# Second products of the attention scores, and the delta rule's exponent rows, over 128 partitions padded with zeros

## The chip, the cores and the metric

The kernel runs on one core of a Trainium2 chip. The metric is the device time of one execution in microseconds (us). TensorE (PE in the profile) multiplies out of SBUF into PSUM. VectorE (DVE), ScalarE (ACT) and GpSimd (POOL) do the rest, and SyncE (SP) issues most of the transfers.

## The reference, cut to what matters

The program is two blocks of a network on 512 tokens of 1024 features: recurrence with forgetting attention, dilated and sliding attention, two cross attentions, MLPs, a gated delta rule, native sparse attention and two layers of experts, all in float32. The change touches two kinds of product in it.

```python
# forgetting, dilated, sliding and sparse attention: heads of 64 features, blocks of 128 queries
sc = jnp.einsum("bqhd,bkhd->bhqk", q[:, q0:q1], k[:, :q1]) * scale
...
p = jax.nn.softmax(jnp.where(mask, sc + bias, -jnp.inf), axis=-1)
outs.append(jnp.einsum("bhqk,bkhd->bqhd", p, v[:, :q1]))
...
# gated delta rule: the factors of a chunk's scores
decay = jnp.exp(jnp.where(causal, gc[..., :, None] - gc[..., None, :], -jnp.inf))
a_strict = einsum('bhncd,bhnsd->bhncs', k_beta, k) * decay
qk = einsum('bhncd,bhnsd->bhncs', q, k) * decay
```

## The kernel before, in words

A float32 value that goes through TensorE is kept as two parts, the rounded value and the rest. Linear layers (`lin_f`, `lin_1`, lines L151 to L153) contract 128 features at a time with three products of parts.

Attention works on one head and 128 queries at a time (j = 0 to 7: four blocks of queries in descending order, two heads). `q_parts` lays a head's rounded queries on one half of the 128 partitions of a tile Q and their rest on the other half. `k_parts` writes the rounded keys to both halves of K, so that one product over 128 partitions gives (rounded query + rest) times rounded key. The rounded query times the key's rest is a second product. Before the change the rests of two heads lie in one tile KL, each on its own 64 partitions, and this product contracts 64 partitions only:

```python
a = slice(e * 64, e * 64 + 64)
return [(Q[e][:, qs], K[e][:, ks]), (Q[e][a, qs], L[a, ks])]
```

`probs` (L294) issues these products into a PSUM bank of tag s (three banks), with a third product over 128 partitions (`crx` with `at`) in forgetting attention. VectorE then takes the minimum (L299, L300) and ScalarE the exponential with its sum (L302, out P). `pv` transposes P on TensorE (L310, into a bank o), copies it (L789 on VectorE or L787 on ScalarE, out PT), and multiplies it with the values (L314, into a bank pt).

The stages with this attention are `ab` (forgetting, 4 pairs of heads), `cd` (dilated and sliding, 8) and `nsa` (8 chunks in two branches, the selected blocks and the window): 32, 64 and 128 second products. The keys seen are 512, 384, 256 or 128 columns. Cross attention (`xa`) has heads of 256 features and contracts 128 partitions in every product.

In `gdn_group` (four groups) each of 4 chunks and 2 heads adds exponent rows to the mask in PSUM by a product that contracts 40 partitions, `gsel` with `rows` (L986, both named g_r in the trace): 32 products in all. Eight partitions from 0 and eight from 32 carry data and the rest are zeros.

The order on each engine comes from a list scheduler at build time, which runs the projections of the next pair of heads between the steps of the present one. Tiles are in rings by tag: x has 16 tiles of 1024 columns, t six of 512, h four. An engine keeps its order, so an instruction that waits holds all behind it.

Of the kernel before, what the change touches and what calls it, by code (L numbers as in the profile page):

```python
# [15 lines left out]
# tiles of the activations by tag: bytes of a row / 2048, and how many; each tag is a queue of its own  # L16
BUFS = {"t": 6, "x": 16, "h": 4, "y": 10, "P": 3, "PT": 3, "bc": 2, "ws": 4, "wh": 3, "wl": 3}
BANKS = {"lin": 2, "pt": 1, "s": 3, "o": 2}
S = 512
# [4 lines left out]
# the experts in the order they are computed in: three of each group of four, then the last of each  # L24
# [9 lines left out]
class Kern:  # L34
# [57 lines left out]
    def tconst(self, name, tag="y"):  # L92
        """A constant of [128, n] that lives in the tiles of the activations, until its last use."""
        src = self.A[name]
        n = src.shape[1]
        x = (self.t(name) if tag == "t" else self.T(name))[:src.shape[0], :n]
        self.nc.sync.dma_start(x, src)
        return x
# [17 lines left out]
    def raw(self, src):  # L116
        """A weight as it is, in the tiles of the weights."""
        self.uid += 1
        x = self.wp.tile([128, 1024], F32, tag="ws", name=f"raw_{self.uid}", bufs=BUFS["ws"])[:src.shape[0], :src.shape[1]]
        self.nc.sync.dma_start(x, src)  # L120
        return x
# [13 lines left out]
    def wap(self, name, kt, cols, off=0):  # L135
        """Pieces (tiles of rows, parts) of a weight that is laid out as [chunk][128][kt * cols]."""
# [11 lines left out]
    def mm3(self, out, a, b, start, stop):  # L148
        """out += a^T b from parts (h, l) of both."""
        mm = self.nc.tensor.matmul  # L150
        mm(out, a[0], b[0], start=start, stop=False)  # L151
        mm(out, a[0], b[1], start=False, stop=False)  # L152
        mm(out, a[1], b[0], start=False, stop=stop)  # L153

    def lin_f(self, w, chunks, xs, evac, N=S, cols=128):
        """Feature-major: evac(c, psum [cols, N]) for each chunk of columns."""
# [6 lines left out]
    def lin_t(self, w, chunks, xs, evac, cols=256, N=S):  # L163
        """Token-major: evac(c, t, psum [128, cols]) for each chunk and tile of tokens."""
# [11 lines left out]
    def lin_s(self, name, cols, xs, evac, put):  # L176
        """A few columns, by token: evac(dst [cols, S], psum), then put(t, psum [128, cols])."""
# [9 lines left out]
    def rms_prep(self, hT, gcol, N=S, scaled=True):  # L187
        """Split parts of h * g by tile, and a function that returns the root mean square's inverse by token and as
        a row on every partition, worked out at its first call."""
# [37 lines left out]
    def rsqrt(self, x, n):  # L227
        """1 / sqrt(x) of a small tile, x > 0: a guess from its bits and three steps of Newton's method."""
# [15 lines left out]
    def bcast(self, r, nt):  # L244
        """[128 tokens, nt] -> [128, nt * 128]: each token's value on every partition."""
# [11 lines left out]
    def q_parts(self, y, name="Q", scale=1.0):  # L257
        """Of each head a tile: its queries times scale, the rounded part where the head lies in y, the rest on the
        other 64 partitions."""
# [9 lines left out]

    def k_parts(self, y, L, name="K", tag="x"):  # L270
        """Of each head a tile with its rounded keys twice; the rest, as it lies in y, to L."""
        K = self.pair(name, tag, F32R)
        for e in range(2):
            a = slice(e * 64, e * 64 + 64)
            for b in range(2):
                self.nc.scalar.activation(K[e][b * 64:b * 64 + 64], y[a], AF.Copy)
            self.nc.vector.tensor_tensor(L[a], y[a], rd(K[e][a]), op=OP.subtract)
        return K

    def qk(self, Q, K, L, e, qs, ks):  # L280
        """The products of head e's queries and keys: of both parts with the rounded keys, and of the rounded
        queries with the keys' rest."""
        a = slice(e * 64, e * 64 + 64)
        return [(Q[e][:, qs], K[e][:, ks]), (Q[e][a, qs], L[a, ks])]

# [1 line left out]
    def probs(self, qk, nk, strip, mn, den, extra=None, floor=None):  # L287
        """exp(logits - max) of 128 queries, [128, nk], with the sums in den."""
# [35 lines left out]
    def pair_out(self, ob, ys):  # L324
        """The transpose of two heads' features of all the tokens, split, into ys; the tiles of tokens in descending
        order."""
# [6 lines left out]
    def out_f(self, name, off, ys, halves=(0, 1), chunks=range(8)):  # L333
        """The residual plus ys^T W, in two halves of ys: the first of them need not wait for the second."""
# [27 lines left out]
    def ab(self):  # L362
# [18 lines left out]
        # log of the forget gate, cumulated  # L381
# [16 lines left out]
        # the cumulated logs of 8 heads as seen from each tile of queries, 32 partitions each: the rounded parts and  # L398
        # after them the rest
        cr, (crh, crl) = self.t("cr"), self.rpair("crx")  # L400
# [13 lines left out]
        def proj(i):  # L414
            if i % 2 == 0:
                self.KL = self.rpair("KL")
            L = self.KL[i % 2]

            def ev(n, p):
                y = self.t("qk")  # L420
                if n < 8:
                    nc.vector.scalar_tensor_tensor(y, p, -0.125, rms()[1], op0=OP.mult, op1=OP.mult)
                    parts[i] = [self.q_parts(y), None, L]
                else:
                    nc.vector.tensor_tensor(y, p, rms()[1], op=OP.mult)
                    parts[i][1] = self.k_parts(y, L)
# [33 lines left out]
    def conv4(self, u, wc, bc):  # L460
        """Causal depthwise convolution of width 4."""
# [9 lines left out]
    def lru(self, uc):  # L471
        nc, vec, V = self.nc, self.vec, VCOL
        # 2 softplus(-lam) = -2 log sigmoid(lam), with a guard for very negative lam
# [12 lines left out]
        for j in range(4):  # L486
# [8 lines left out]
            # i * u, and b = (1 + a) s = 1 - a, with a = (1 - s) / (1 + s)  # L495
# [11 lines left out]
    def gelu(self, g):  # L507
        """2 gelu, tanh form."""
# [10 lines left out]
    def lru_out(self, hs, g, ys):  # L519
        """The scan's result times the gate."""  # L520
# [4 lines left out]
    def cd(self):  # L525
# [34 lines left out]
        def proj_k(i, n):  # L560
            if i % 2 == 0:
                self.KL = self.rpair("KL")
            L = self.KL[i % 2]

            def ev(n, p):
                kp[i] = self.k_parts(rotated(p, 1.0), L), L
# [13 lines left out]
        def sliding(i):  # L580
            """Heads i and i + 4, with sinks."""
# [48 lines left out]
    def mem_prep(self):  # L630
        """The memory, and a function that works out its root mean square's inverse."""
# [37 lines left out]
    def xa(self, l):  # L669
# [19 lines left out]
        for hp in range(2):  # L689
            # the transposed weights of two heads, in parts: [128 keys, block of keys, token]  # L690
# [81 lines left out]
    def row_const(self, name, n):  # L772
        """A row of a kernel input on every partition."""
# [9 lines left out]
    def copy(self, out, in_):  # L783
        """A copy out of PSUM by the scalar and the vector engine in turn."""
# [6 lines left out]
    def gdn(self):  # L791
# [4 lines left out]
        # a and b of each token and head  # L796
# [15 lines left out]
        # softplus(a) = max(a, 0) + log(1 + exp(-|a|)), the rounding of 1 + exp taken back  # L812
# [18 lines left out]
        # per token and head: beta / 2, -beta exp(gc), exp(gc), exp(gl - gc), gc; per head exp(gl);  # L831
        # rho: the exponents of a row of the scores, gc + log beta and gc
# [13 lines left out]
        # keys and queries are kept as 2 silu(), their norms go into the exponents and the factors  # L846
# [5 lines left out]
        self.grows, self.gsel = (self.cp.tile([40, n], F32R, tag=f"g_r{n}", name=f"g_r{n}") for n in (256, 8))  # L852
        nc.scalar.activation(self.grows, self.gcst[:40, :256], AF.Copy, scale=0.0)
        nc.vector.tensor_tensor(self.gsel, rd(self.identr[:40, 0:8]), rd(self.identr[:40, 32:40]), op=OP.add)
        # the scores and the inverses of a group, its 8 matrices with rows of 128 and one more between them
# [43 lines left out]
    def gdn_group(self, grp):  # L899
# [8 lines left out]
        def conv_silu(p, tile_no, s):  # L908
            """s = 2 silu(conv(p))"""
# [17 lines left out]
        ss = self.small((128, 16), "ss", tag="gA", bufs=3)  # (keys, queries) x chunk x head  # L927
# [26 lines left out]
        # the inverse norms, in the factors and the exponents of this group  # L954
# [14 lines left out]
        # a row of a chunk and head: its exponents, the rounded parts and 32 partitions further the rest  # L969
# [3 lines left out]
        self.split(pr[:8, :256], rows[:8], rows[32:])  # L973

        # B (strictly upper, [s, c]) and the masked scores, by chunk
        B_, Q_ = self.T("B"), self.T("Q")
        B, Q = u4(B_), u4(Q_)
        for n in range(NT):
# [4 lines left out]
            for i in range(2):  # L983
                u = 2 * n + i
                nc.tensor.matmul(pe[:, i * 256:(i + 1) * 256], self.identr, self.gmask, start=True, stop=False)
                nc.tensor.matmul(pe[:, i * 256:(i + 1) * 256], self.gsel[:, u:u + 1].to_broadcast([40, 128]), rows, start=False, stop=True)  # L986
# [6 lines left out]
        # X = (I + B)^-1 and its transpose: the blocks of 16 on the diagonal, each on a partition, then twice as many  # L993
        # each time
# [14 lines left out]
        for b in (2, 4, 8):  # L1009
            # of the blocks of 2 b on the diagonal, the quarter (i, k): [64, block, rows, columns]  # L1010
# [65 lines left out]
        # the chunks in turn  # L1076
# [53 lines left out]
    def out_moe(self, wname, ys, layer, out=None):  # L1130
        """alpha R + ys^T W, its layer norm, and the mixture of experts with the norm after it."""
# [7 lines left out]
        def part(c, k, tag=None):  # L1139
            """The rows of four tiles from k on of the weight's chunk c."""  # L1140
# [14 lines left out]
        if cut:  # L1155
            # the first four tiles of ys need not wait for the others
# [9 lines left out]
        # the norm's gain and offset, for the residual; those of the experts' inputs are put in by feature  # L1166
# [6 lines left out]
        def logits(t, hf):  # L1173
            """The router's products with half of the features of z, before its norm."""
# [12 lines left out]
        def stats(t):  # L1187
            """The inverse of the deviation, and minus the mean times it."""
# [7 lines left out]
        def norm(t, r, m):  # L1196
            """z normalised, and the logits with it."""
# [824 lines left out]
```

## Time and profile before

| | |
|---|---|
| median of 3 runs | 2955.98 us (2948.23 to 2966.57) |
| the profiled execution, first to last instruction | 2954.5 us |
| TensorE busy | 2778.2 us (94%) |
| VectorE, ScalarE, GpSimd busy | 1792.6, 1371.4, 218.9 us |
| mean granted TensorE clock | 0.965 of full speed |

The profile gives no other time for the profiled execution than its span, which lies 1.5 us below the median. A busy TensorE is not TensorE at its peak: a matmul counts as busy from its start to the modelled end of its pipeline, so neighbours overlap. How close products follow each other is read from their start times.

### The profile page before, as it was taken

The numbers are of one execution on the slowest core, as the hardware profiler recorded it, in microseconds if no ns is written. First come the engines' busy times: TensorE is split into PE (matmuls) and PEld (weight loads), VectorE is DVE, ScalarE is ACT, GpSimd is POOL, SyncE is SP. The second block draws the span as 40 slices with busy tenths as digits, with TensorE's granted clock in tenths as the row PEclk, the third lists the DMA queues.
The fourth block names the chain that finished last, engine by engine and source line by source line (L and its number), as shares of the span: only waits on it lengthen the run. The fifth ranks groups of instructions, "written<-read, shape, count | busy, mean of one in ns | idle before, by whom it ended". The sixth has DMA issues, their size and how long they took to land. (4 is left out here: it accounts for less than half of the span.)

```text
span 2954.5 us, 40039 instructions
## 1 busy us (share of the span) xinstructions
PE 2778.2 (94%) x15088; PEld 2322.6 (79%) x15088; DVE 1792.6 (61%) x3539; ACT 1371.4 (46%) x2545; POOL 218.9 (7%) x181
## 2 busy tenths in 40 slices
PE   8999999999999999999999999969959999996995
PEld 6788888888877988888877889958848777785873
DVE  6765553444366556445357776677674566568767
ACT  5654442233355435333246443347752554324774
POOL 1101010000110011000010000020020000002001
PEclk9999999999999999999999999979989999797997
DMA  4314133333222422335333223237873101013876
GB/s 137 95 53 144 49 105 99 96 97 100 83 76 68 129 72 79 95 98 176 100 96 108 75 60 95 72 122 262 267 263 110 50 30 58 8 37 112 274 253 217
DMA packets 123111, 333.65 MB, mean 113 GB/s; under 512 B 21780, under 2 KB 37812, under 8 KB 122904
## 3 DMA queue, kind: packets, MB, share of 16 engines
q1 hardware_dynamic: 120472, 322.48, 34.8%
q0 software_dynamic: 2432, 8.46, 0.8%
q8 instruction: 124, 2.03, 0.3%
q14 instruction: 83, 0.68, 0.1%
HBM read 301.49 MB, written 29.07 MB: 112 GB/s over the span
## 5 line engine op out<-in xcount | busy, mean ns | idle before, releaser
L130 ACT ACTIVATE wh<-ws 128x1024 fp32r<-128x1024 f32 (+2 forms) x521 | 534.2, 1030 | 887.4 <-PE lin L152 606.1
L131 DVE TENSOR_TENSOR wl<-ws,wh 128x1024 fp32r<-128x1024 f32 (+2 forms) x521 | 622.9, 1201 | 229.1 <-ACT wh L130 225.5
L151 PE MATMUL lin<-xs,wh 128*128 128x512 f32 (+2 forms) x1080 | 428.4, 397 | 7.5 <-ACT xs L196 6.1
L152 PE MATMUL lin<-xs,wh 128*128 128x512 f32 (+2 forms) x1080 | 428.0, 396 | 1.8 <-DVE xs L197 1.8
L153 PE MATMUL lin<-xs,wl 128*128 128x512 f32 (+2 forms) x1080 | 427.2, 396 | 0.5 <-DVE wl L131 0.5
L151 PEld LDWEIGHTS lin<-xs,wh 128*128 128x128 f32 (+2 forms) x1080 | 202.1, 187 | 52.8 <-ACT xs L196 6.8
L152 PEld LDWEIGHTS lin<-xs,wh 128*128 128x128 f32 (+2 forms) x1080 | 202.0, 187 | 45.7 <-DVE xs L197 4.5
L153 PEld LDWEIGHTS lin<-xs,wl 128*128 128x128 f32 (+2 forms) x1080 | 202.1, 187 | 43.2 <-issue 1.2
L344 DVE TENSOR_TENSOR h<-lin,h 128x512 f32<-128x512 f32 x112 | 77.4, 691 | 248.5 <-PE lin L153 248.4
L151 PE MATMUL lin<-sr,wh 128*128 128x512 f32 x512 | 199.2, 389 | 0.0
L152 PE MATMUL lin<-sr,wh 128*128 128x512 f32 x512 | 199.2, 389 | 0.0
L153 PE MATMUL lin<-sr,wl 128*128 128x512 f32 x512 | 199.2, 389 | 0.0
L302 ACT ACTIVATE P<-s,mn 128x256 f32<-128x256 f32 (+1 forms) x224 | 114.3, 513 | 74.7 <-DVE mn L300 70.0
L739 DVE SCALAR_TENSOR_TENSOR ra<-lin,bc 128x512 f32<-128x512 f32 x64 | 44.3, 692 | 166.8 <-PE lin L153 164.3
L1525 PE MATMUL o<-oh,Rh 128*128 128x256 f32 x512 | 132.2, 291 | 6.8 <-PEq L1386 4.9
L1525 PE MATMUL o<-oh,Rl 128*128 128x256 f32 x512 | 130.8, 288 | 4.5 <-PEq L1386 3.6
L152 PE MATMUL s<-wl,exh 128*128 128x512 f32 x256 | 106.5, 416 | 13.0 <-DVE wl L131 12.9
L151 PE MATMUL s<-wh,exh 128*128 128x512 f32 x256 | 102.9, 405 | 9.8 <-ACT wh L130 9.7
L151 PEld LDWEIGHTS lin<-sr,wh 128*128 128x128 f32 x512 | 96.1, 188 | 20.0
L153 PEld LDWEIGHTS lin<-sr,wl 128*128 128x128 f32 x512 | 96.1, 188 | 19.9
L152 PEld LDWEIGHTS lin<-sr,wh 128*128 128x128 f32 x512 | 96.1, 188 | 19.8
L1525 PEld LDWEIGHTS o<-oh,Rh 128*128 128x128 f32 x512 | 100.4, 196 | 12.2 <-DVE oh L1514 6.9
(604 smaller groups left out, 6282.9 us busy)
## 6 DMA issues: line engine op xcount, KB each, us to landing
ws<-in_moe_wgu SPq DMA_DIRECT2D x128, 512.0 KB, 5.2
ws<-in_mlp_wu SPq DMA_DIRECT2D x64, 512.0 KB, 3.6
ws<-in_mlp_wd SPq DMA_DIRECT2D x64, 512.0 KB, 3.5
ws<-in_moe_wd SPq DMA_DIRECT2D x64, 512.0 KB, 5.4
yd<-ey SPq DMA_DIRECT2D x60, 256.0 KB, 4.5
ws<-in_gdn_w SPq DMA_DIRECT2D x24, 512.0 KB, 3.6
ws<-in_ab_w SPq DMA_DIRECT2D x16, 512.0 KB, 3.9
ws<-in_xa_wk SPq DMA_DIRECT2D x16, 512.0 KB, 3.7
```

Source lines behind the costliest of these rows:

```text
L130: nc.scalar.activation(wh, ws, AF.Copy)
L131: nc.vector.tensor_tensor(wl, ws, rd(wh), op=OP.subtract)
L151: mm(out, a[0], b[0], start=start, stop=False)
L152: mm(out, a[0], b[1], start=False, stop=False)
L153: mm(out, a[1], b[0], start=False, stop=stop)
L302: nc.scalar.activation(P[:, :nk], p[:, :nk], AF.Exp, bias=mn, scale=-1.0, accum_out=den)
L344: self.nc.vector.tensor_tensor(self.hT[n], p, self.hT[n], op=OP.add)
L739: nc.vector.scalar_tensor_tensor(a, p, 0.0, rms()[1], op0=OP.max, op1=OP.mult)
L1525: nc.tensor.matmul(p[:, j * 256:(j + 1) * 256], Rs[t][i][:, f * 128:(f + 1) * 128], oh[:, t], start=t + i == 0, stop=t == NT - 1 and i == 1)
```

## The change

The keys' rests get a tile for each head, and the 64 partitions that are not the head's are set to zero by GpSimd. The second product then takes all 128 partitions of Q, of which the half with the queries' rest meets zeros. `rows` and `gsel` become 128 partitions high, and the new ones hold zeros. The pairs KL are now allocated for each pair of heads with K, instead of one for two pairs of heads. `crx` leaves the ring x for two tiles of the ring t.

```diff
-    def k_parts(self, y, L, name="K", tag="x"):
-        K = self.pair(name, tag, F32R)
+    def k_parts(self, y, name="K", tag="x"):
+        nc = self.nc
+        K, L = self.pair(name, tag, F32R), self.pair("KL", tag, F32R)
         for e in range(2):
-            a = slice(e * 64, e * 64 + 64)
+            a, z = slice(e * 64, e * 64 + 64), slice(64 - e * 64, 128 - e * 64)
+            nc.gpsimd.memset(rd(L[e][z]), 0.0)
             for b in range(2):
-                self.nc.scalar.activation(K[e][b * 64:b * 64 + 64], y[a], AF.Copy)
-            self.nc.vector.tensor_tensor(L[a], y[a], rd(K[e][a]), op=OP.subtract)
-        return K
+                nc.scalar.activation(K[e][b * 64:b * 64 + 64], y[a], AF.Copy)
+            nc.vector.tensor_tensor(L[e][a], y[a], rd(K[e][a]), op=OP.subtract)
+        return K, L
...
-        a = slice(e * 64, e * 64 + 64)
-        return [(Q[e][:, qs], K[e][:, ks]), (Q[e][a, qs], L[a, ks])]
+        return [(Q[e][:, qs], K[e][:, ks]), (Q[e][:, qs], L[e][:, ks])]
...
-        cr, (crh, crl) = self.t("cr"), self.rpair("crx")
+        cr, crh, crl = self.t("cr"), self.t("crh", F32R), self.t("crl", F32R)
...
-            if i % 2 == 0:
-                self.KL = self.rpair("KL")
-            L = self.KL[i % 2]
...
-        self.grows, self.gsel = (self.cp.tile([40, n], F32R, tag=f"g_r{n}", name=f"g_r{n}") for n in (256, 8))
+        self.grows, self.gsel = (self.cp.tile([128, n], F32R, tag=f"g_r{n}", name=f"g_r{n}") for n in (256, 8))
...
-                nc.tensor.matmul(pe[:, i * 256:(i + 1) * 256], self.gsel[:, u:u + 1].to_broadcast([40, 128]), rows, start=False, stop=True)
+                nc.tensor.matmul(pe[:, i * 256:(i + 1) * 256], self.gsel[:, u:u + 1].to_broadcast([128, 128]), rows, start=False, stop=True)
```

The number of products and their columns stay. In `cd`, `nsa` and the delta rule the order on TensorE, VectorE and ScalarE stays too, apart from names. It moves at two places.

On VectorE in `ab`, during the attention of the second pair of heads, the rests of the third pair's keys (KL) stand behind the last of the five minima (L299) before:

```order
L299 TENSOR_REDUCE mf_1392<-s_1387 128x1
L300 ISA s_1403,mn_1292<-s_1403,c_fstrip_843 128x128
L300 ISA mn_1292 128x1
L300 ISA s_1387,mn_1292<-s_1387,c_fstrip_843,mf_1392 128x128
L300 ISA mn_1292 128x1
L277 TENSOR_TENSOR KL_1213<-qk_1283,K_1285 64x512 x2
```

And in the changed kernel, whose lines are shifted by some (L277 is L280, L299 is L301, L300 is L302):

```order
L301 TENSOR_REDUCE mf_1308<-s_1303 128x1
L131 TENSOR_TENSOR wl_1900<-ws_1898,wh_1899 128x1024
L280 TENSOR_TENSOR KL_1291<-qk_1288,K_1290 64x512
L302 ISA s_1303,mn_1300<-s_1303,c_fstrip_844,mf_1308 128x128
L302 ISA mn_1300 128x1
L280 TENSOR_TENSOR KL_1291<-qk_1288,K_1290 64x512
L301 TENSOR_REDUCE mf_1328<-s_1323 128x1
```

The rests now stand at the first minimum of that pair of heads. TensorE's order is rearranged over some 70 instructions at the same place, with the same products.

On GpSimd in `cd`, before, the products of the rotation (L536, zr, one for each projection of queries or keys) follow each other:

```order
L536 TENSOR_TENSOR zr_6531<-zr_6531,CS_6109 128x512
L536 TENSOR_TENSOR zr_6580<-zr_6580,CS_6109 128x512
L536 TENSOR_TENSOR zr_6627<-zr_6627,CS_6109 128x512
L536 TENSOR_TENSOR zr_6676<-zr_6676,CS_6109 128x512
L536 TENSOR_TENSOR zr_6850<-zr_6850,CS_6109 128x512
```

In the changed kernel (where they are L534) the zeros of a pair of heads stand ahead of the rotation of its keys:

```order
L277 MEMSET KL_6552 64x512
L534 TENSOR_TENSOR zr_6541<-zr_6541,CS_6120 128x512
L534 TENSOR_TENSOR zr_6593<-zr_6593,CS_6120 128x512
L277 MEMSET KL_6651 64x512
L277 MEMSET KL_6651 64x512
L534 TENSOR_TENSOR zr_6640<-zr_6640,CS_6120 128x512
L534 TENSOR_TENSOR zr_6692<-zr_6692,CS_6120 128x512
L277 MEMSET KL_6876 64x512
```

Five pairs of such settings stand among the thirteen products of the rotation, and 26 settings in the whole program.

## Rows read from the trace of the kernel before

**Rows 1.** The page: busy time, share and instructions of each engine.

```profile
PE 2778.2 (94%) x15088; PEld 2322.6 (79%) x15088; DVE 1792.6 (61%) x3539; ACT 1371.4 (46%) x2545; POOL 218.9 (7%) x181
```

**Rows 2.** Stretches: us; busy PE, PEld, DVE, ACT, POOL (instructions); clock, DMA, GB/s.

```profile
123.00:202.00 79.00, 77.70 (x448) 60.93 (x448) 57.80 (x167) 49.27 (x123) 6.97 (x7) 1.00 0.12 36
338.00:360.00 22.00, 21.95 (x153) 19.79 (x152) 17.50 (x46) 13.95 (x46) 0.00 (x0) 1.00 0.04 13
823.00:1016.00 193.00, 191.27 (x1152) 159.92 (x1152) 128.86 (x283) 107.11 (x252) 15.83 (x11) 0.95 0.30 88
1590.00:1797.00 207.00, 202.72 (x1227) 168.57 (x1227) 150.59 (x335) 97.25 (x272) 5.54 (x6) 1.00 0.22 64
2313.00:2605.00 292.00, 286.70 (x1632) 229.43 (x1632) 175.59 (x572) 132.77 (x371) 23.75 (x42) 0.91 0.09 29
2313.00:2526.00 213.00, 212.13 (x1272) 167.83 (x1271) 136.71 (x441) 105.39 (x289) 18.43 (x31) 1.00 0.11 38
2526.00:2554.00 28.00, 25.41 (x99) 20.97 (x99) 12.14 (x42) 9.62 (x29) 0.98 (x4) 0.51 0.00 1
```

**Rows 3.** Tile KL, whole program: count and shapes; idle before it until (us, times).

```profile
L294 PE MATMUL s<-KL,Q x224: 322/410/792, 123.0 to 2604.4; 64*128 64x256 f32 x36, 64*128 64x128 f32 x28, 64*128 64x512 f32 x24, 64*128 64x384 f32 x24
...
  issue: 28.1, 123
```

**Rows 4.** Timeline of TensorE in `nsa`: start, us, then the product.

```profile
2337.95 0.43 PE L294 MATMUL s<-KL,Q 64*128 64x384 f32 x1
2338.32 0.39 PE L294 MATMUL s<-K,Q 128*128 128x256 f32 x1
2338.63 0.38 PE L294 MATMUL s<-KL,Q 64*128 64x256 f32 x1
2338.95 0.38 PE L294 MATMUL s<-K,Q 128*128 128x256 f32 x1
...
2345.40 0.31 PE L294 MATMUL s<-K,Q 128*128 128x128 f32 x1
2345.64 0.33 PE L294 MATMUL s<-KL,Q 64*128 64x128 f32 x1
2345.89 0.33 PE L310 MATMUL o<-c_ident,P 128*128 128x128 f32 x1
...
2348.18 0.48 PE L294 MATMUL s<-K,Q 128*128 128x512 f32 x1
2348.59 0.49 PE L294 MATMUL s<-KL,Q 64*128 64x512 f32 x1
2349.01 0.50 PE L294 MATMUL s<-K,Q 128*128 128x512 f32 x1
```

**Rows 5.** Timeline of TensorE in linear layers: 256 and 512 columns over 128 partitions.

```profile
240.06 0.28 PE L152 MATMUL lin<-wl,mx 128*128 128x256 f32 x1
240.18 0.28 PE L153 MATMUL lin<-wh,mx 128*128 128x256 f32 x1
...
249.17 0.40 PE L152 MATMUL lin<-y,wh 128*128 128x512 f32 x1
249.40 0.39 PE L153 MATMUL lin<-y,wl 128*128 128x512 f32 x1
```

**Rows 6.** Timeline of TensorE: 16 products over 64 partitions in the delta rule.

```profile
1646.43 1.14 PE L1049 MATMUL s<-Y,B 64*64 64x64 f32 x16
```

**Rows 7.** Timeline of TensorE: exponent rows of the delta rule.

```profile
1590.61 0.38 PE L986 MATMUL s<-g_r,g_r 40*128 40x256 f32 x1
1590.92 0.51 PE L152 MATMUL lin<-xs,wh 128*128 128x512 f32 x1
```

**Rows 8.** Waits of TensorE in `nsa` (2313 to 2605): us in total, times, longest.

```profile
PE o L310 <- ACT P L302: 5.1, 3, 2.9
```

**Rows 9.** Timeline of TensorE in `nsa`: the longest of those waits, in brackets.

```profile
2528.59 0.69 PE L310 MATMUL o<-c_ident,P 128*128 128x128 f32 x2 [2.93 <-ACT P L302]
```

**Rows 10.** GpSimd by line and shape: setting a tile of 1024 columns.

```profile
L1058 POOL MEMSET Z<- 128x1024 f32 x8 | 7.4, 952 | 237.7 <-PE s L1049 219.4 <-PE pt L1863 18.4
```

More of the change, by code (lines that the diff above doesn't have):

```diff
@@ L422, in ev @@
                     nc.vector.scalar_tensor_tensor(y, p, -0.125, rms()[1], op0=OP.mult, op1=OP.mult)
-                    parts[i] = [self.q_parts(y), None, L]
+                    parts[i] = (self.q_parts(y),)
                 else:
                     nc.vector.tensor_tensor(y, p, rms()[1], op=OP.mult)
-                    parts[i][1] = self.k_parts(y, L)
+                    parts[i] += self.k_parts(y)
             self.lin_f(w, (4 + i, 8 + i), xs, ev)
@@ L560, in proj_k @@
         def proj_k(i, n):
-            if i % 2 == 0:
-                self.KL = self.rpair("KL")
-            L = self.KL[i % 2]
             def ev(n, p):
-                kp[i] = self.k_parts(rotated(p, 1.0), L), L
+                kp[i] = self.k_parts(rotated(p, 1.0))
             self.lin_f(w, [n], xs, ev)
@@ L851, in gdn @@
         nc.scalar.activation(self.gmask, self.gcst[:, 192:448], AF.Copy)
-        self.grows, self.gsel = (self.cp.tile([40, n], F32R, tag=f"g_r{n}", name=f"g_r{n}") for n in (256, 8))
-        nc.scalar.activation(self.grows, self.gcst[:40, :256], AF.Copy, scale=0.0)
-        nc.vector.tensor_tensor(self.gsel, rd(self.identr[:40, 0:8]), rd(self.identr[:40, 32:40]), op=OP.add)
+        self.grows, self.gsel = (self.cp.tile([128, n], F32R, tag=f"g_r{n}", name=f"g_r{n}") for n in (256, 8))
+        nc.scalar.activation(self.grows, self.gcst[:, :256], AF.Copy, scale=0.0)
+        nc.vector.tensor_tensor(self.gsel, rd(self.identr[:, 0:8]), rd(self.identr[:, 32:40]), op=OP.add)
         self.bdram, self.xdram = ([self.dp.tile([8 * 129, 128], F32, tag=f"{n}{i}", name=f"{n}{i}")[:] for i in range(2)] for n in "bx")
@@ L972, in gdn_group @@
             nc.tensor.transpose(pr[:8, k * 128:(k + 1) * 128], rho[:, k * 8:(k + 1) * 8], self.ident)
-        self.split(pr[:8, :256], rows[:8], rows[32:])
+        self.split(pr[:8, :256], rows[:8], rows[32:40])
         B_, Q_ = self.T("B"), self.T("Q")
@@ L1656, in proj_k @@
         def proj_k(j):
-            tag = "hx"[j]
-            L = self.pair("KL", tag, F32R)
             kk = [None] * 2
             def ev(n, p):
-                br = (n - 4) // 2
-                kk[br] = self.k_parts(p, L[br], "K", tag), L[br]
+                kk[(n - 4) // 2] = self.k_parts(p, "K", "hx"[j])
             self.lin_f(w, (4 + j, 6 + j), xs, ev)
```

## The prediction

> **What bounds the kernel now.** I read the page first: TensorE is busy for 94% of the span, and no other engine for more than 61% [rows 1]. A share over the whole program says little of the stages that change, so next came the view of stretches: forgetting attention (123 to 202), dilated and sliding attention with the next stage's memory keys (823 to 1016), the delta rule's scores and what lies between (1590 to 1797), and sparse attention (2313 to 2605). In each TensorE is busy for 98 to 99%, VectorE for 60 to 73% [rows 2]. So TensorE sets their length, unless its busy time hides gaps. It does hide them. The view of tile KL lists the 224 second products of the scores, and says that the weight load of 123 of them came after idle time which nothing but the engine's own issue ended [rows 3]. The timeline shows what that costs: with 512 columns, K starts at 2348.18, KL at 2348.59, the next K at 2349.01, so 0.41 and 0.42 us apart [rows 4]. In a linear layer products of 512 columns over 128 partitions are 0.23 us apart, and those of 256 columns 0.12 us [rows 5]. Second products have the same columns and engine, but 64 partitions in place of 128.
>
> Is it the number of partitions, or the change of it? Sixteen products in a row over 64 partitions take 1.14 us together, at most 0.07 us each [rows 6]. So products over 64 partitions are not slow among their own kind. What costs is the step from 128 to 64 and the step back. The kernel makes both for nearly every second product, because the first product, the transposes and the values all use 128.
>
> **The change part by part.** *The steps between 128 and 64 partitions go.* For each shape I add what lies before and behind a KL, and take off what two products of 128 partitions need:
> - 512 columns: 0.41 + 0.42 - 2 x 0.23 = 0.37 us [rows 4, 5].
> - 384 columns: the step behind is 0.37 us (2337.95 to 2338.32), and I take the one ahead as equal. Without the step it would be half-way between 0.12 and 0.23, an estimate from rows 5: 2 x (0.37 - 0.175) = 0.39 us.
> - 256 columns: 0.31 + 0.32 - 2 x 0.12 = 0.39 us.
> - 128 columns: 0.24 + 0.25 = 0.49 us, against at most 2 x 0.12, since they can't take longer than 256: 0.25 us.
>
> The program has 48, 48, 72 and 56 of these (the 224 of rows 3, by `nk` in the code): `ab` and `nsa` the same number of each shape, 8 and 32, and `cd` 8, 8, 32 and 16. So `ab` has 8 x (0.37 + 0.39 + 0.39 + 0.25) = 11.2 us, `nsa` four times that, 44.8 us, and `cd` 8 x 0.37 + 8 x 0.39 + 32 x 0.39 + 16 x 0.25 = 22.6 us: 78.6 us together. The 32 exponent rows of the delta rule show the same step: 0.31 us behind one of 256 columns over 40 partitions [rows 7], as behind a KL. At 0.39 us each they hold 12.5 us. On TensorE that makes 91 us.
>
> *How much of it reaches the end.* The other engines must follow faster. The bound from above is all of it. Cross attention (338 to 360) has the same chain of scores, minimum, exponential, transposes and values, all over 128 partitions. There TensorE is busy for 21.95 of 22 us while VectorE is at 80% [rows 2]. After the change VectorE's work would fill 175.59 / (292 - 44.8) = 71% of `nsa` and 128.86 / (193 - 22.6) = 76% of `cd`, both less than there. In `ab` it would be 57.80 / (79 - 11.2) = 85%, which is more than any row shows beside a full TensorE. The bound from below is half, which I choose for the case that copies of PT and exponentials come too late for the shorter gaps: TensorE already waits 5.1 us for P in `nsa` [rows 8]. I take half in `ab` (5.6 us) and 85% elsewhere (0.85 x 79.9 = 67.9 us), nearer to the row of cross attention: 73 us.
>
> *The clock.* The granted clock is at 0.95 on average in `cd` and 0.91 in `nsa`, elsewhere among these stages at 1.00 [rows 2]. With two levels, 2.4 and 1.2 GHz, that is 0.05 x 2 x 193 = 19 us and 0.09 x 2 x 292 = 53 us at the lower. From 2526 to 2554 it is at half, with 99 products in 28 us, 3.9 for each busy us, against 1272 / 213 = 6.0 in the stretch ahead at the full clock [rows 2]. Just where that begins TensorE idles 2.93 us until P comes from ScalarE [rows 9]. Such a wait is not removed; with less work on TensorE it may grow. Denser products behind it may bring the clock back sooner. If all 72 us ran at full clock, 72 x (1 - 3.9 / 6.0) = 25 us would be won. If two more stretches like this one came, 2 x 28 x 0.35 = 20 us would be lost. I take zero, since the waits that stand at the start remain, and keep both ends.
>
> *What is added.* Twenty-six settings of 64 x 512 go to GpSimd. A setting of 1024 columns takes 0.952 us [rows 10], so one of 512 columns is some 0.48 us, an estimate, and the sum 12.4 us on an engine that is busy for 7% [rows 1]. They cost nothing while the pair's weights and projection run on other engines: a projection of 24 products of 512 columns lasts 24 x 0.23 = 5.5 us, and the pair of settings 0.96. The zeros stand ahead of the rotation of the keys in `cd`, on a queue that keeps its order. If that cover went, five pairs of settings would delay five rotations, 5 x 0.96 = 4.8 us, and the wait of a setting for its place in ring x would come on top. That place is free once the products of the pair of heads before the last are done, and the keys K of the same pair need one then, too. Moving `crx` to ring t and KL to one tile for each pair lets the third pair's rests in `ab` be written some twenty instructions earlier on VectorE; that stage's gain is already halved for VectorE, so I add none. Weight loads for all partitions, the larger `gsel` and `rows`: none, as each is one instruction for one.
>
> The sum, on the profiled execution: 2954.5 - 73 = 2881.5 us. Its span is 1.5 us below the median of the runs, so I forecast 2883 us for the median.
>
> **The rivals.** *The step costs are not of the partitions (2956 us).* The trace has no score product of 128 partitions with a rest tile, so the gap could belong to something else in it, such as the operands' parts. Then all the spacing stays, and 0 to 5 us are added by the settings. For it: the loads' idle time has no releaser [rows 3]. Against it: the exponent rows, with other tiles and other operands, show the same 0.31 us [rows 7], and the third kind of product, 64 partitions among themselves, shows none of it [rows 6]. The Trainium skill's page "TensorE: Matmul & The Clock Gate", in the section "Why this matters for your kernels", says that one product over 32 partitions takes the same time as one over 128, and that something is won only by running small ones side by side; by that, padding wins nothing, and the time would be this rival's, 2956 us. The Trainium skill's page "TensorEngine Tiling (Array Packing)", under "Key Properties", has the opposite for this place: a change of the tiling mode empties the engine; by that, the sum above holds. The trace sides with the second page: 0.41 us against 0.23 [rows 4, 5].
>
> *TensorE waits instead (about 2920 us).* All the gaps go, but the chain through VectorE and ScalarE sets the pace, and less than half arrives. For it: gaps stand between a transpose and the product that needs its copy, so they cover the copy. Against it: cross attention keeps TensorE full [rows 2]. At 40% of 91 us the time is 2956 - 36 = 2920 us.
>
> *Slower, by the clock (about 2998 us).* With waits for P in every pair of heads, the clock could stay at 1.2 GHz through sparse attention. Its 213 us at the full clock [rows 2] would then take 213 x 6.0 / 3.9 = 328 us, 115 more, and less the 73 that is 42 more than before: 2998 us. It becomes slower than before once some 73 / 0.54 = 135 us of work that now runs at the full clock (0.54 = 6.0 / 3.9 - 1) falls to the lower one. For it: the lower clock is found in these stages, beside such waits [rows 2, 9]. Against it: products get denser, not sparser, wherever no wait comes.
>
> **How the numbers follow.** The forecast, with between 50% and all of the 91 us, has a chance of 0.75: 2956 - 91 = 2865 to 2956 - 46 = 2910, and by the clock's ends 25 us less or 20 more. Waits instead has 0.12, no effect 0.09, slower 0.04. The range leaves out no effect, slower, and the far ends of the clock: 2848 to 2926. A difference of 1%, some 30 us, is about what a measurement of this kernel can tell from no change. Faster by over 1% means below 2926: the forecast's 0.75 and three quarters of the waits' case, 0.84. Within 1%: 0.12. Slower: 0.04.
>
> **What would show it right or wrong.** In the trace after, K and KL of 512 columns should start 0.23 us apart and the next product another 0.23 later; the 28.1 us of idle time by issue ahead of KL's loads should be near zero; `nsa` should last about 255 us in place of 292, and `cd` about 174 in place of 193. Right on the steps but wrong on the time would be a sum of waits for P or PT in `nsa` well above 5.1 us. Wrong on the clock would be more than 72 us at 1.2 GHz in `cd` and `nsa` together. The forecast fails if the spacing stays at 0.41, or if waits of zr on GpSimd behind the settings appear in `cd`.

## The result and the profile after

The changed kernel takes 2874.1 us in the median of four runs (2868.6 to 2876.4), against 2956.7 in the median of four runs of the kernel before: a ratio of 0.971, with a 95% interval of 0.969 to 0.974. So 82.6 us are gone, where the forecast had 73. The profiled execution has a span of 2870.8 us.

The busy times of the page answer to [rows 1]:

```profile
PE 2684.3 (94%) x15088; PEld 2290.8 (80%) x15088; DVE 1783.8 (62%) x3539; ACT 1368.9 (48%) x2545; POOL 231.1 (8%) x207
```

TensorE has the same 15088 instructions and is busy for 94 us less. Its share is still 94%, so the share alone would have told nothing. GpSimd has 26 instructions more, the settings.

The stretches answer to [rows 2], with the same columns: forgetting attention, dilated and sliding attention, delta rule, sparse attention.

```profile
124.00:198.00 74.00, 68.77 (x449) 59.26 (x447) 58.25 (x167) 49.19 (x122) 8.76 (x11) 1.00 0.12 37
819.00:992.00 173.00, 168.82 (x1153) 152.60 (x1154) 123.57 (x284) 107.15 (x253) 19.05 (x17) 0.97 0.34 99
1565.00:1763.00 198.00, 193.78 (x1234) 165.75 (x1232) 150.79 (x336) 96.20 (x273) 5.52 (x6) 1.00 0.23 67
2281.00:2520.00 239.00, 230.63 (x1632) 207.12 (x1630) 171.60 (x570) 132.48 (x368) 25.77 (x45) 0.98 0.12 39
```

They are 5, 20, 9 and 53 us shorter, 87 together. The rest of the program is 3 us longer. Two more things are to be seen. First, TensorE's idle time in the four (length less busy) has grown from 12.6 us to 22.0. Second, the mean granted clock of sparse attention rose from 0.91 to 0.98. With two levels, the time at half clock is (1 - clock) x 2 x length: 10 us in the second stretch and 10 in the fourth, against 19 and 53.

Tile KL (count: least, median and longest ns) answers to [rows 3] and, by its settings, to [rows 10]:

```profile
L296 PE MATMUL s<-KL,Q x224: 272/334/562, 124.6 to 2519.6; 128*128 128x256 f32 x36, 128*128 128x128 f32 x28, 128*128 128x512 f32 x24, 128*128 128x384 f32 x24
L277 POOL MEMSET KL<- x26: 517/519/524, 99.5 to 2347.4; 64x512 f32 x26
```

The 28.1 us of idle time by the engine's own issue have no line any more. The timeline of TensorE in sparse attention shows why, and answers to [rows 4]:

```profile
2312.16 0.47 PE L296 MATMUL s<-K,Q 128*128 128x512 f32 x1
2312.48 0.40 PE L296 MATMUL s<-KL,Q 128*128 128x512 f32 x1
2312.71 0.40 PE L296 MATMUL s<-K,Q 128*128 128x512 f32 x1
2312.95 0.39 PE L296 MATMUL s<-KL,Q 128*128 128x512 f32 x1
2313.17 0.40 PE L152 MATMUL lin<-lx,wh 128*128 128x512 f32 x1
```

K, KL, K, KL and the linear layer's product behind them start 0.22 to 0.24 us apart, as in a linear layer. Only the first K is 0.32 us ahead of its KL; it follows short products of 64 columns. Over all shapes, by the starts at the full clock, the median from K to KL and from KL to the next product is 0.25 and 0.23 us with 512 columns, 0.18 and 0.18 with 384, 0.15 and 0.12 with 256, 0.14 and 0.14 with 128. The 0.15 lies between two groups of about the same size, 0.12 us and 0.20 us, and these lines have both:

```profile
2332.72 0.61 PE L312 MATMUL o<-c_ident,P 128*128 128x128 f32 x4
2333.09 0.36 PE L296 MATMUL s<-K,Q 128*128 128x256 f32 x1
2333.29 0.28 PE L296 MATMUL s<-KL,Q 128*128 128x256 f32 x1
2333.41 0.29 PE L296 MATMUL s<-K,Q 128*128 128x256 f32 x1
2333.53 0.28 PE L296 MATMUL s<-KL,Q 128*128 128x256 f32 x1
```

With 256 columns, a K that follows transposes of 128 columns, or products of 64, has its KL 0.20 us behind it; a K that follows products of 256 columns or more has it 0.12 us behind, in 26 of 28 places.

The long waits of TensorE for P in sparse attention answer to [rows 8, 9], three in all with 5.3 us before the transposes L312. These are the longest two in the timeline (the wait in brackets), and the stretch at half clock behind each in the view of stretches:

```profile
2469.18 0.97 PE L312 MATMUL o<-c_ident,P 128*128 128x128 f32 x4 [3.13 <-ACT P L304]
2498.66 0.66 PE L312 MATMUL o<-c_ident,P 128*128 128x128 f32 x4 [1.88 <-ACT P L304]
...
2469.00:2473.00 4.00, 3.82 (x19) 3.72 (x20) 2.78 (x9) 2.52 (x9) 0.00 (x0) 0.57 0.02 4
2500.00:2507.00 7.00, 7.00 (x36) 7.00 (x36) 3.53 (x12) 2.60 (x9) 0.00 (x0) 0.51 0.28 77
```

The kernel before has the same two. Its first, of 2.93 us, is [rows 9], with half clock from 2526 to 2554 [rows 2]; its second, from the same views:

```profile
2572.39 0.66 PE L310 MATMUL o<-c_ident,P 128*128 128x128 f32 x4 [1.81 <-ACT P L302]
...
2574.00:2598.00 24.00, 24.00 (x93) 19.76 (x91) 8.91 (x28) 6.34 (x20) 0.00 (x0) 0.50 0.07 23
```

So the waits have not gone, and have not grown by more than 0.2 us; but behind them the clock is back after 3 and 7 us instead of 27 and 24.

These two waits stand before the same products in both kernels, whose order in sparse attention is the same. So they cut the stage, from its first second product to its last, into three parts with the same work. First the kernel before, then the changed one, with the columns of [rows 2]:

```profile
2312.98:2528.59 215.61, 212.15 (x1273) 167.85 (x1272) 139.25 (x452) 106.65 (x293) 19.41 (x34) 0.99 0.11 37
2528.59:2572.39 43.80, 41.96 (x210) 34.67 (x211) 21.11 (x74) 15.40 (x46) 2.96 (x6) 0.71 0.00 1
2572.39:2604.40 32.01, 32.01 (x147) 26.39 (x147) 14.64 (x45) 10.20 (x33) 1.28 (x1) 0.63 0.06 17
...
2281.87:2469.18 187.31, 181.39 (x1272) 160.53 (x1270) 136.35 (x452) 106.48 (x293) 21.54 (x38) 1.00 0.14 46
2469.18:2498.66 29.48, 27.30 (x210) 25.97 (x210) 20.33 (x73) 15.62 (x46) 2.96 (x6) 0.94 0.01 1
2498.66:2519.61 20.95, 20.80 (x146) 20.07 (x147) 14.16 (x45) 9.55 (x30) 1.27 (x1) 0.84 0.10 26
```

The first part has 99 of the stage's 128 second products and next to no half clock in either kernel. It is 28.3 us shorter, 0.29 us for each second product. The other two have 29 and are 25.4 us shorter together, where 0.29 us each would make 8. The other 17 us go with 39 us less at half clock.

### The profile page after: what moved, and what is told of

Read it like the earlier page. It is cut to its first block, busy times and chain, and to the rows that moved or that the text cites. A ratio compares the mean times of both kernels' runs of the same rounds, so it can differ in the third digit from the quotient of the medians.

```text
span 2870.8 us, 40089 instructions
## 1 busy us (share of the span) xinstructions
PE 2684.3 (94%) x15088; PEld 2290.8 (80%) x15088; DVE 1783.8 (62%) x3539; ACT 1368.9 (48%) x2545; POOL 231.1 (8%) x207
## 5 line engine op out<-in xcount | busy, mean ns | idle before, releaser
L152 PE MATMUL s<-wl,exh 128*128 128x512 f32 x256 | 106.2, 415 | 12.7 <-DVE wl L131 12.6
```

## The experiments

The theory: the products over 64 or 40 partitions cost a step on both sides because the engine changes between two arrangements, and the number of partitions alone decides that. The rivals: the tiles, rings and settings did it; any change of the number of partitions costs; each product over 64 costs, whether the number changes or not; or the clock holds most of the gain.

**The scores alone and the exponent rows alone.** In the first run the exponent rows of the changed kernel are back at 40 partitions, in the second only they are widened in the kernel before:

```diff
-        self.grows, self.gsel = (self.cp.tile([128, n], F32R, ...
+        self.grows, self.gsel = (self.cp.tile([40, n], F32R, ...
```

> The changed kernel with the delta rule's exponent rows back at 40 partitions; the scores keep 128. If each step between 64 or fewer and 128 partitions costs its 0.19 us and the two parts of the change are independent, the delta rule's stage from 1565.7 to 1762.4 us grows by some 10 us again (32 products at 0.39 us, most of it arriving) and the time is 2884 us, ratio to before 0.975. If the gain came from the scores' stages alone (rings, clock), the time is that of the changed kernel, 2874 us.

> The kernel before with only the delta rule's exponent rows over 128 partitions. No tile moves between rings and nothing is set to zero on GpSimd more than before, so this is the widening alone. Steps: 10 us less than before, 2946 us, ratio 0.9965, and the next product 0.12 us after the one of 256 columns in place of 0.31. If widening itself wins nothing, 2956 us and still 0.31 us.

Measured: 2882.9 us for the scores alone (ratio 0.9745, 0.972 to 0.977) and 2946.0 for the rows alone (0.996, 0.994 to 0.998), against 2957.3 before, on the same chip for both. So the scores bring 74 us and the rows 11, together some 86, and the whole change brings 83. In the timeline of the rows alone, the first lines of the delta rule answer to [rows 7]:

```profile
1587.52 0.28 PE L986 MATMUL s<-g_r,g_r 128*128 128x256 f32 x1
1587.63 0.39 PE L152 MATMUL lin<-xs,wh 128*128 128x512 f32 x1
```

0.11 us to the next product, in place of 0.31. The two parts act each for itself.

**All of the change but the width.** Tiles, rings, zeros and settings as in the changed kernel; the second products take the head's 64 partitions of them, and the exponent rows are at 40:

```diff
-        return [(Q[e][:, qs], K[e][:, ks]), (Q[e][:, qs], L[e][:, ks])]
+        a = slice(e * 64, e * 64 + 64)
+        return [(Q[e][:, qs], K[e][:, ks]), (Q[e][a, qs], L[e][a, ks])]
```

> The changed kernel's tiles, rings and settings to zero, but the second products take 64 partitions again and the exponent rows 40: all of the change except the width. Steps: nothing is won, 2952 to 2960 us, ratio 0.999 to 1.002, and K to KL of 512 columns 0.41 us apart. If the layout of the rings (KL for each pair, crx out of ring x) had a part in the gain, it shows here, most in forgetting attention: up to 5 us less.

Measured: 2957.8 us, a ratio of 1.001 (0.999 to 1.003). Its timeline in sparse attention:

```profile
2350.89 0.47 PE L297 MATMUL s<-K,Q 128*128 128x512 f32 x1
2351.29 0.49 PE L297 MATMUL s<-KL,Q 64*128 64x512 f32 x1
2351.71 0.69 PE L297 MATMUL s<-K,Q 128*128 128x512 f32 x1
```

The spacing of 0.40 and 0.42 us is back, and with it all of the time. The rival of tiles and rings falls. The run also prices the 26 settings: nothing that this measurement can tell.

**96 and 72 partitions in place of 128.** In the changed kernel the second product of each pair's first head takes 96 partitions and that of the second head 128; the exponent rows take 72:

```diff
-        return [(Q[e][:, qs], K[e][:, ks]), (Q[e][:, qs], L[e][:, ks])]
+        a = slice(0, 96) if e == 0 else slice(0, 128)
+        return [(Q[e][:, qs], K[e][:, ks]), (Q[e][a, qs], L[e][a, ks])]
```

> The changed kernel, but the first head of each pair takes 96 partitions in its second product and the exponent rows take 72. If the cost comes with any change of the number of partitions, half of the scores' gain (39 us at most, some 32 arriving) and all of the delta rule's (10 us) are lost: some 2916 us. If it comes only with products of 64 partitions or fewer, the time is that of the changed kernel, 2874 us, ratio 0.9715.

Measured: 2872.2 us, 0.971 (0.969 to 0.973), the same as with 128. In its timeline the product over 96 stands between two over 128:

```profile
2314.58 0.40 PE L297 MATMUL s<-KL,Q 96*128 96x512 f32 x1
2314.81 0.39 PE L297 MATMUL s<-K,Q 128*128 128x512 f32 x1
2315.04 0.39 PE L297 MATMUL s<-KL,Q 128*128 128x512 f32 x1
```

0.23 us to either side. So it is no change of the number that costs, but the change between more than 64 partitions (72, 96 and 128 behave alike) and at most 64 (40 and 64 do). The Trainium skill's page "TensorEngine Tiling (Array Packing)", under "Available Configurations", lists modes of 128, 64 and 32 rows and none between; by that, 72 and 96 belong to the mode of 128, and these runs agree.

**Each second product as two halves in a row.** In the kernel before, its columns are split into two products, so there are 224 products more but no step more:

```diff
-            nc.tensor.matmul(p[:, :nk], q, k, start=i == 0, stop=i == len(qk) - 1)
+            for c in ((0, nk // 2), (nk // 2, nk)) if i == 1 else ((0, nk),):
+                nc.tensor.matmul(p[:, c[0]:c[1]], q, k[:, c[0]:c[1]], start=i == 0, stop=i == len(qk) - 1 and c[1] == nk)
```

> The kernel before, with each second product of the scores (64 partitions) split by columns into two that follow each other. The number of steps stays, the number of products over 64 partitions doubles. If the cost is of the step, the second half follows the first at the pace of products of one kind: 0.11 to 0.12 us for 256 columns, and the time is at most 224 x 0.05 us = 11 us more, 2956 to 2967 us. If every product over 64 partitions pays, 224 x 0.35 us = 78 us more, 3034 us.

Measured: 2989.9 us, 1.012 (1.010 to 1.014), 33 us more, between the two. The timeline in sparse attention, where x2 joins the two halves, and the three attention stretches:

```profile
2350.23 0.36 PE L295 MATMUL s<-K,Q 128*128 128x256 f32 x1
2350.53 0.43 PE L295 MATMUL s<-KL,Q 64*128 64x128 f32 x2
2350.89 0.38 PE L295 MATMUL s<-K,Q 128*128 128x256 f32 x1
...
124.00:215.00 91.00, 88.48 (x473) 71.74 (x471) 59.39 (x166) 48.58 (x122) 7.59 (x7) 0.89 0.11 36
838.00:1040.00 202.00, 201.87 (x1212) 172.19 (x1211) 127.20 (x280) 106.46 (x249) 14.80 (x11) 0.92 0.29 85
2338.00:2648.00 310.00, 308.24 (x1747) 254.03 (x1747) 174.65 (x571) 132.91 (x370) 23.71 (x42) 0.87 0.08 26
```

From KL to the next K it is 0.36 us with two halves and 0.32 with one [rows 4]. By the median starts the split costs nothing per KL with 512 columns, 0.03 us with 384, 0.05 with 256, 0.08 with 128: 48 x 0.03 + 72 x 0.05 + 56 x 0.08 = 10 us in all, not the 78 of a full price for each product. But one expectation missed: the second half does not follow at the pace of products of one kind. With 256 columns in each half it starts 0.22 us behind the first, not 0.11 to 0.12:

```profile
2337.94 0.50 PE L295 MATMUL s<-KL,Q 64*128 64x256 f32 x2
2338.16 0.28 PE L295 MATMUL s<-KL,Q 64*128 64x256 f32 x1
2338.37 0.50 PE L152 MATMUL lin<-lx,wh 128*128 128x512 f32 x1
```

The first of these lines joins both halves; the second is the second half alone. So some 0.1 us is left between two products over the same 64 partitions, without a change of the number. The run excludes the full price for each product, but not a smaller one; why it is there was not tried. The rest of the 33 us is largely found in the clock. The profiled execution was the slowest of the six, 46 us over the one before. Its three stretches are 39 us longer, and half clock makes up 20, 32 and 81 us of them, 133 in place of 72. At the 35% that [rows 2] show to be lost there, 61 us more are 21, which with the 10 of the split leaves 8 of the 39 without an account. In the second stretch TensorE was busy for 201.87 of 202 us, at a mean granted clock of 0.92.

**The scores of two heads in turn.** In the kernel before, both heads' first products are written ahead of both heads' second products:

```diff
+    def scores(self, qks, nk):
+        ps = [self.psum("s") for _ in qks]
+        for i in range(len(qks[0])):
+            for p, qk in zip(ps, qks):
+                self.nc.tensor.matmul(p[:, :nk], *qk[i], start=i == 0, stop=i == len(qk) - 1)
+        return ps
```

> The kernel before, with the scores of two heads issued in turn: first products of both, then the second products of both. The heads lie on different halves of the partitions. Where both find a bank (about one pair in four), two products over 64 partitions on different halves follow each other. If the step is between numbers of partitions, not between halves, the second of them starts at most 0.23 us after the first for 512 columns, against 0.41 before. If a change of the half costs the same, 0.41 us. Time: some 10 us less than before where pairs form, if the new order costs nothing.

> The same kernel as the pairs run (the kernel before, the logits of two heads issued in turn), timed against the kernel before on one chip: 2915 to 2926 us by its single time of 2921. In its trace some 45 pairs of second products start 3 ns apart, one head's on the upper and one on the lower 64 partitions. By the steps 45 x (0.39 us + about 0.13 us for the product that runs beside the other) = 23 us of the 36 is theirs, and the rest the half clock in the attention stages, which fell from 72 to about 44 us.

Measured: 2920.7 us in a single execution, and when timed 2926.0 us, 0.991 (0.988 to 0.993): 29 us less than before. The timeline of the timed run, in dilated attention:

```profile
844.76 0.61 PE L292 MATMUL s<-K,Q 128*128 128x512 f32 x2
845.30 0.50 PE L292 MATMUL s<-KL,Q 64*128 64x512 f32 x2
845.73 0.45 PE L292 MATMUL s<-K,Q 128*128 128x384 f32 x1
```

Two second products of 512 columns together take as long as one before, 0.43 us to the next K. Tile KL shows why: both last 498 ns and start 3 to 4 ns apart, one head's on the lower, the other's on the upper 64 partitions; they run beside each other. The trace has 42 such pairs. The first of these two expectations was too small in time. At the spacing measured for each shape (further down), 12 pairs of 512, 17 of 256 and 13 of 128 columns hold 13 us of steps, and products beside others some 6; half clock in the attention fell from 72 to 51 us, at 35% another 7. That makes 26 of the 29 us, as an estimate. The Trainium skill's page "TensorEngine Tiling (Array Packing)", under "Key Properties", says that different tiles of the array work in parallel, and its page "TensorE: Matmul & The Clock Gate", under "The mechanism", gives some 4 ns between their starts; the trace agrees, with 3 to 4.

**The same order with 128 partitions.** The edit above, in the changed kernel.

> The changed kernel, with the logits of two heads issued in turn as in the pairs run of the kernel before: first both heads' products over the latent dims, then both heads' second products, over 128 partitions each. If what the pairs run gained (36 us) was steps between 128 and 64 partitions and the two halves running at once, there is nothing of it left to gain here: 2874 us, at most 10 to either side by the order of the waits. If it gained because TensorE waits less for the exponentials, the 25 us or so of waits in the changed kernel's attention stages fall as well, and this run takes 2850 to 2860.

Measured: 2873.5 us, 0.973 (0.970 to 0.976): no gain over the changed kernel. So what the order gained lay in the steps, the halves and the clock that goes with them, not in shorter waits for the exponentials, and nothing of it is left where the steps are gone.

**TensorE filled.** Ahead of each logits tile, extra products over 128 partitions into the same bank, overwritten by the first real one; once in the changed kernel, once in the kernel before:

```diff
+        q, k = qk[0]
+        for n in {512: (512, 384), 384: (384, 384), 256: (256, 256, 256), 128: (128, 128)}[nk]:
+            nc.tensor.matmul(p[:, :n], q, k[:, :n], start=True, stop=True)
```

> The changed kernel with the time of the steps filled by products: before each first product of the scores, two or three of the same operands over 128 partitions into the same bank, which the first product then overwrites (0.40, 0.35, 0.36 and 0.22 us for 512, 384, 256 and 128 columns; 76 us in all against 79 us for the steps). The result is unchanged. If only TensorE's time counts, the gain of the scores is gone: 2874 + 72 = 2946 us. If a part of the gain was the clock's, which falls less where TensorE has more columns, the time stays below that by as much: down to 2928 us, with fewer than 72 us at half clock in the attention stages.

> The kernel before, with the same extra products over 128 partitions ahead of each logits tile as the filled run had in the changed kernel (about 70 us of products by that run's trace, overwritten, so the output is not touched). In the changed kernel they cost 78 us, with 20 us of half clock in the attention stages to win back at most 10 from. Here those stages have 72 us at half clock, about 28 us of excess more than in the changed kernel by the spacing of their products. If the changed kernel's gain holds a clock part, filling raises the clock here too and gives it back: 3005 to 3015 us. If the clock has no part in it, the filling costs what it costs in the changed kernel: 3030 to 3036 us.

Measured: 2952.6 us in the changed kernel (0.999, 0.998 to 1.001), 78.5 more than without; 3035.1 in the kernel before (1.028, 1.024 to 1.031), 80.5 more. The three attention stretches of the first, then of the second:

```profile
122.00:211.00 89.00, 82.94 (x525) 71.80 (x523) 59.40 (x168) 49.96 (x124) 9.24 (x11) 0.98 0.12 36
832.00:1028.00 196.00, 190.08 (x1316) 170.22 (x1314) 126.16 (x284) 107.71 (x253) 20.86 (x17) 1.00 0.29 89
2311.00:2594.00 283.00, 275.49 (x1898) 245.08 (x1896) 174.17 (x569) 133.19 (x371) 24.92 (x46) 0.99 0.09 31
```

```profile
124.00:219.00 95.00, 92.87 (x525) 73.06 (x524) 59.94 (x168) 50.28 (x124) 7.29 (x7) 0.98 0.11 34
843.00:1051.00 208.00, 207.10 (x1310) 173.99 (x1310) 127.78 (x280) 107.29 (x251) 16.52 (x11) 1.00 0.28 83
2354.00:2687.00 333.00, 329.34 (x1912) 262.19 (x1911) 177.00 (x572) 133.66 (x371) 22.82 (x42) 0.94 0.07 24
```

The first run says that a us more of TensorE is a us more of these stages: they grew by 82 us, their busy time by 80. (Its profiled execution is 72.5 us longer in all.) What is taken off TensorE need not arrive as fully: in the changed kernel TensorE idles 9.4 us more. The second was to show a clock part by a smaller cost, 50 to 60 us, and did not: it left 44 of the 72 us at half clock, so it could give back only 28 x 0.35 = 10 us, and the filling of the changed kernel, where 10 of 20 us were left, gave back 3 or 4 as well. In the stretches the filling did cost 10 us less than in the changed kernel (72 against 82), but the totals don't show that, and each is uncertain by some 5 to 10 us. On the clock this pair is inconclusive.

## Why the prediction was right

*What bounds the kernel* held: TensorE sets these stages, and the filled run shows it from the other side.

*The steps* held in kind and nearly in size. All but the width of the products changes nothing; 72 and 96 partitions do what 128 do. One reading was too wide: "not slow among their own kind" holds for the row it was read from, products of 64 columns [rows 6], but the second halves above follow the first 0.22 us apart with 256 columns, where products over 128 partitions need 0.12. The spacing by shape, before less after, both sides of a KL, is 0.36 us with 512 columns (forecast 0.37), 0.36 with 384 (0.39), 0.34 with 256 (0.39) and 0.21 with 128 (0.25): 48 x 0.36 + 48 x 0.36 + 72 x 0.34 + 56 x 0.21 = 71 us instead of 78.6. The forecast took the pace of linear layers, 0.12 and 0.23 us, for what is left without the step. That pace is reached behind long products, but a K behind transposes or products of 64 columns keeps its KL 0.20 us off with 256 columns and some 0.3 with 512. The exponent rows alone brought 11.3 us instead of 12.5. So TensorE had some 82 us to give, not 91.

*How much of it arrives* by stage: `ab` 5 us (forecast 5.6), `cd` 20 (0.85 x 22.6 = 19.2), the delta rule 9 (0.85 x 12.5 = 10.6). Three of four are right within the reading of the stretches. In `ab` the reason given, VectorE and ScalarE too late for the shorter gaps, is in the waits for P, from 1.3 us to 4.6; over the four stretches TensorE idles 9.4 us more. `nsa` gained 53 us where 0.85 x 44.8 = 38.1 were forecast, more than all its steps by my own count. The three parts of the stage say how: 28 + 8 = 36 us came with the steps, near the forecast, and 17 with the clock.

*The clock* is the term that was mis-sized: I took zero between 25 us gained and 20 lost. My reason was that the waits at the start of the slow stretches remain. They do, but the length of a stretch is not set by the wait ahead of it: behind waits of 3.13 and 1.88 us the clock was back after 3 and 7 us, where with the steps it had stayed low for 27 and 24. The prediction has a sentence for it ("Denser products behind it may bring the clock back sooner"), and I gave it no weight. Half clock in `cd` and `nsa` fell from 72 us to 20. At 35%, 52 us less are 18, of which `nsa` has 0.35 x 43 = 15. The three parts of `nsa` have 17 us for 39 us less, 0.44 us for each. The runs give the price apart from the steps: in 47 executions of the kernel before, timed beside these runs, the time at half clock, from span and mean clock of each, goes from 177 to 225 us, and the span rises by 0.41 us with each us of it (95% interval 0.36 to 0.46), with the same steps and the same work in all. It averages 203 us there and 164 in the four runs of the changed kernel: 39 x 0.41 = 16 us of the 82.6. Over the four stretches, as an estimate, 71 + 11 of steps and 18 of clock, less 9.4 of idle time, are 91 us against 87. Half clock goes with the steps in the other runs too: by their stretches, `nsa` has 53 and 40 us of it in the two that keep the scores' steps (rows alone, all but the width), 14 and 10 us in the two that lack them (scores alone, 96 and 72). What about the steps keeps the clock low is not shown.

That the total is off by only 10 us is in part luck: the sum of the steps was too high by 9 us, the idle time took 9.4 us where 18 had been allowed for it, which cancels that, and the clock, taken as zero, gave 16 to 18.

*What is added* cost nothing, as taken. A setting lasts 0.52 us (estimate 0.48). In `cd` GpSimd's settings do wait for their place in ring x, and rotations (L534) now wait behind keys' rests that they had not waited for, as this view of GpSimd's waits in that stretch shows (us, times, longest):

```profile
POOL zr L534 <- DMA zr<-z: 48.7, 6, 11.5
POOL zr L534 <- DVE mn L302: 15.0, 2, 12.3
POOL zr L534 <- DVE KL L280: 12.9, 2, 7.6
POOL zr L534 <- ACT P L304: 12.4, 1, 12.4
POOL KL L277 <- PE s L296: 3.0, 2, 2.6
```

I had named such waits as a sign of failure. They are not: the rotations' idle time for their DMA, 111.5 us before by the same view, fell by 63 us, more than the other four lines hold together (43 us); TensorE's one wait in `cd` for what the rotation feeds, a tile Q, is 0.4 us after 0.9 before; and `cd` lasts 173 us, forecast 174. A wait off the path was a poor thing to test by.

*The rivals.* "Not of the partitions" (2956 us) is excluded by the runs with all but the width and with the rows alone. The Trainium skill's page "TensorE: Matmul & The Clock Gate", in the section "Why this matters for your kernels", would have had padding win nothing; the measurement, 82.6 us, is against it in this mixed stream of products. "TensorE waits instead" came in at the size of 9.4 us, not 50. "Slower, by the clock" failed at its point of decision: in the four stages no more work fell to the lower clock; its time there went down by 52 us.

## What to carry to other kernels

Where products over at most 64 partitions alternate with products over more, look at the starts of successive products, not at the busy share: each change cost some 0.19 us here, and zeros up to more than 64 partitions took it away at the price of a few cheap settings. If products of 64 partitions must stay, put those of the two halves next to each other, so that they run side by side and share the step (over the same half they do not run side by side, and the second still came some 0.1 us late); with every product padded, that order brings nothing more. Count the time at half clock as a term of its own: here it cost some 0.4 us for each us, and TensorE, with the steps gone, got its clock back earlier behind an unchanged wait.

## What was not expected of the hardware

- Two products over different halves of the partitions started 3 to 4 ns apart, in 42 places; the program only put them next to each other.
- 72 and 96 partitions cost what 128 do (2872.2 against 2874.1 us); the price sets in somewhere between 72 partitions and 64.
- Two products over the same 64 partitions, 256 columns each, started 0.22 us apart, against 0.12 over 128 partitions, though the number of partitions did not change between them.
- A TensorE that was busy for 201.87 of 202 us was granted 0.92 of its clock in the run with halves. Half clock is not found only in idle stretches: from 2574 to 2598 before, too, it was busy for all 24 us, though a wait of 1.81 us stands just ahead. The steps are part of such busy time, since a product counts as busy to its modelled end.
